# Second feed-forward of a decoder block on Trainium2: the output of hidden tiles 4 to 15 by seven block products, with three of seven low weight parts made by ScalarE and adding transfers

## The chip, the cores and the metric

One core of a Trainium2 chip runs the whole kernel. Its engines work from queues of their own and wait for each other through semaphores: TensorE (PE: matmuls out of SBUF into PSUM; PEld: its weight loads), VectorE (DVE), ScalarE (ACT), GpSimd (POOL) and SyncE (SP, which issues nearly all transfers). The metric is the device time of one execution in microseconds (us). The kernel before was timed three times: 1016.45, 1017.04 and 1017.88 us.

## The reference, cut

```python
def swiglu(u, w_in, w_out):
    a, b = jnp.split(u @ w_in, 2, axis=-1)
    return (jax.nn.silu(a) * b) @ w_out

    ...
        u = modulate(rmsnorm(h, g_norm_ffn1[l]), sh1, sc1)
        h = h + 0.5 * gt1 * swiglu(u, w_ffn1_in[l], w_ffn1_out[l])
        u = modulate(rmsnorm(h, g_norm_mix[l]), sh2, sc2)
        h = h + gt2 * token_mixing(u, cos, sin, w_in[l], w_pool[l], pool_scale[l],
                                   w_pool_branch[l], w_attn_branch[l], w_out[l])
        u = modulate(rmsnorm(h, g_norm_ffn2[l]), sh3, sc3)
        h = h + 0.5 * gt3 * swiglu(u, w_ffn2_in[l], w_ffn2_out[l])
    return rmsnorm(h, g_final)
```

There are 512 tokens of width 1024, and the hidden width of each feed-forward is 2816, all in float32. The change is in the second feed-forward alone, in the product with `w_out`, and in how the weights of its block products are split.

## The kernel before

**Layout.** Everything is held transposed: features on the 128 partitions, the 512 tokens along the row. The residual stream is eight tiles `H` of 128 x 512, the hidden layer 22 tiles.

**Three matmuls for one.** TensorE multiplies in a format with fewer bits than float32 (fp32r), so that each operand is split into a high and a low part and a product is made of three matmuls: high by high, high by low and low by high (`mm3`). For a chunk of weights ScalarE copies the raw chunk into the ring `whi` (the rounding copy is the high part), and VectorE subtracts that from the raw chunk into the ring `wlo`. A chunk has 1024 columns, 512 KB; a ring holds seven of them. The method `split` does this for the chunks in the order of `plan`, and `look(4)` ahead of each product makes sure that the chunk of four products later is in the queues. So ScalarE's and VectorE's queues hold, between the work on one product and that on the next, the split of a chunk that is needed four products later. Raw chunks come by SyncE into five buffers (`raw` and the two upper quarters of `X`).

**Input products.** From hidden tile 4 on, `duo` makes two hidden tiles at a time by Winograd's form of Strassen's scheme: seven block products (`product`, 24 matmuls of 256 columns each) in place of eight. Blocks are the two halves of the 1024 input features, the two halves (a and b of the gated unit) of the output, and the two halves of the tokens. Of the seven weight chunks three are raw ones (the first, fourth and sixth) and four are differences which VectorE makes ahead of them (`make`). A duo uses three PSUM banks A, B, C: after product 0 ScalarE copies A to C, after product 1 it copies B out (`p5`), after products 2 and 4 it copies A out (`u2`, `u3`) while A goes on being added to by products 2, 4 and 6, and after products 3 and 6 it applies silu. The hidden pair h is multiplied together in `mult`, and its high and low parts are made by `high` (ScalarE) and `low` (VectorE), which are put off by one or two products: `later(n, f)` keeps f until `step` has been called n times, and `step` comes once after each product, **ahead of** that product's own copies.

**Output products.** The hidden tiles are used up in five parts, (0, 4), (4, 8), (8, 12), (12, 16) and (16, 22) (`PARTS`). For a part other than the last, `ffn` runs eight output tiles: for each of them 4 x 3 matmuls of 512 columns, then one VectorE instruction that multiplies the bank by the gate and adds it to `H`. Four chunks of 1024 columns serve a part. The order is: part 0; pairs 4, 6 and 8, part (4, 8); pairs 10 and 12, part (8, 12); pairs 14 and 16, part (12, 16); pairs 18 and 20, the last part. So one pair of a part's successor always lies between a part's own hidden tiles and its output; it is called the third pair below.

The order of the instructions is that of the program: no scheduler moves them.

Of the kernel before, what the change touches and what calls it, by code (L numbers as in the profile page):

```python
# [14 lines left out]
P = 128  # L15
# [39 lines left out]

def lay_ffn(w_in, w_out, first, plain):

    ins, outs = [], []  # L60
    if first:
        cols = np.concatenate([c for j in range(first) for c in _tiles(j * P, DFF + j * P)])
        for k in range(KT):
            ins.append(w_in[k * P:(k + 1) * P][:, cols])
    for j in range(first, plain):
        for c in _tiles(j * P, DFF + j * P):
            ins.append(_fmajor(w_in, c))
    for j in range(plain, FT, 2):
        for i, c in ((0, 0), (0, DFF), (1, DFF), (1, 0)):
            rows = w_in[i * D // 2:(i + 1) * D // 2]  # L70
            ins.append(np.concatenate([_fmajor(rows, x) for x in _tiles(c + j * P, c + j * P + P)], axis=1))
    for k0, k1 in PARTS:
        for m in range(KT):
            outs.append(_fmajor(w_out[k0 * P:k1 * P], np.arange(m * P, (m + 1) * P)))
    n = KT * (len(PARTS) - 1)
    return ins, [np.concatenate(outs[i:i + 2], axis=1) for i in range(0, n, 2)] + outs[n:]

# [59 lines left out]
class Kernel:  # L137
# [6 lines left out]
    def plan(self):  # L144
# [11 lines left out]
        self.loads, self.order, self.last = [], [], {}  # L156
        self.shifted = set()

# [6 lines left out]

        def blocks(recs):
            n = len(self.loads)
            self.shifted.update(range(len(self.order), len(self.order) + 7))
            self.loads.extend(recs)
# [13 lines left out]
        def ffn(n, ins, outs, first):  # L183
# [4 lines left out]
            for part, (k0, k1) in enumerate(PARTS):  # L188
                while j < pairs_before(n, part):
# [5 lines left out]
                    else:  # L195
                        blocks(ins[at:at + 4])
                        j, at = j + 2, at + 4
                plain(outs[part * KT // 2:(part + 1) * KT // 2] if part + 1 < len(PARTS) else outs[-KT:])

# [71 lines left out]
    def split_hi(self):  # L271
# [21 lines left out]
        for y, x in parts:  # L293
            self.nc.scalar.activation(self.hi[:, y], r[:, x], AF.Copy)  # L294
        if i + 1 < len(self.order) and self.order[i + 1][3] and self.order[i + 1][1] < self.fetched:
            self.make(i + 1)
# [344 lines left out]
    def ffn_post(self, j, s, pb):  # L641
        nc = self.nc
        h = self.fw.tile([P, T], F32, name=("hf", "u3")[j % 2])
        nc.vector.tensor_tensor(h, s, pb, op=OP.mult)
# [4 lines left out]
    def ffn_silu(self, j, pa):  # L649
        s = self.fw.tile([P, T], F32, name=("sl", "u2")[j % 2])  # L650
        self.nc.scalar.activation(s, pa, AF.Silu)
        return s
# [70 lines left out]
    def duo(self, j, first, last):  # L723
# [12 lines left out]
        s = self.fw.tile([P, 2 * T], F32, name="sl")  # L736
        c = self.fw.tile([P, 2 * T], F32, name="hf")
        u2, u3, p5 = (self.fw.tile([P, T], F32, name=x) for x in ("u2", "u3", "p5"))
        q = lambda x: x.rearrange("p (j h t) -> p j h t", j=2, h=2)
        r = lambda x: x.rearrange("p (j t) -> p j t", j=2)  # L740
        silu = lambda h, bank: nc.scalar.activation(q(s)[:, :, h, :], r(bank), AF.Silu)

# [3 lines left out]
        def high():  # L746
            copy(self.HHall[:, j % NH * T:(j % NH + 2) * T], c)

        def low():
            x = slice(j % NH * T, (j % NH + 2) * T)  # L750
            v.tensor_tensor(self.HLall[:, x], c, self.HHall[:, x], op=OP.subtract)


        for i, (bank, u, start) in enumerate(((A, blk(lo4, T1), True), (B, S[0], True), (A, S[1], False),
                                              (C, blk(hi4, T1), False), (A, S[2], False), (B, S[3], False),
                                              (A, blk(hi4, T2), False))):
            if i == 6:
                v.tensor_tensor(q(c)[:, :, 1, :], r(u3), r(p5), op=OP.add)
            self.look(4)
# [7 lines left out]
            elif i == 1:  # L767
                copy(p5, B)
            elif i == 2:
                copy(u2, A)  # L770
            elif i == 3:
                silu(0, C)
            elif i == 4:
                copy(u3, A)
            elif i == 6:
                silu(1, A)
                v.tensor_tensor(q(c)[:, :, 0, :], r(B), r(u2), op=OP.add)
        if last:
# [3 lines left out]
        else:  # L782
            self.later(1, mult)
            self.later(2, high)
            self.later(2, low)

    def ffn2(self):
        self.put, self.now = [], 0
        bk = [self.nb() for _ in range(4)]
        self.head(2, bk, AF.Silu)  # L790
        self.todo, last = self.u_steps(2)
        do = lambda n: [self.todo.pop(0)() for _ in range(n)]
# [32 lines left out]
    def ffn(self, n, j, last=None):  # L825
# [10 lines left out]
        for part, (k0, k1) in enumerate(PARTS):  # L836
            tail = part + 1 == len(PARTS)
            while j < pairs_before(n, part):
                if j < PLAIN[n]:
                    self.ffn_pair(j, beside)  # L840
                    j += 1
                else:
                    self.duo(j, last, tail and j + 2 == FT)
                    last = None
# [3 lines left out]
            nk = k1 - k0  # L848
            hk = [(self.HH[k % NH], self.HL[k % NH]) for k in range(k0, k1)]
            if not tail:  # L850
                for m in range(0, KT, 2):
# [493 lines left out]
    def build(self):  # L1345
# [39 lines left out]
        with self.open_ffn():  # L1385
            self.ada_pool = ExitStack()
            self.adaw = self.ada_pool.enter_context(tc.tile_pool(name="f1a", bufs=4))
            self.put, self.now = [], 0
            self.startup()
# [134 lines left out]
def lay_inputs(x, c, positions, w_ada, b_ada, g_norm_ffn1, w_ffn1_in, w_ffn1_out, g_norm_mix, w_in, w_pool,  # L1524
# [3 lines left out]
    col = lambda v: A(v).reshape(-1, P).T  # L1528
    f1i, f1o = lay_ffn(A(w_ffn1_in)[0], A(w_ffn1_out)[0], FIRST, PLAIN[0])
    f2i, f2o = lay_ffn(A(w_ffn2_in)[0], A(w_ffn2_out)[0], 0, PLAIN[2])  # L1530
    wp = np.zeros((P, 2 * P), np.float32)
# [32 lines left out]
```

## Time and profile before

| | |
|---|---|
| timed runs | 1016.45, 1017.04, 1017.88 us |
| profiled execution, span from the first to the last instruction | 1018.4 us |
| second feed-forward, first block product to the last part | 734.94 to 973.61 us |
| output of a part (4 to 7, 8 to 11, 12 to 15) | 21.8 us each |
| two pairs between two outputs | 38.5 us |
| loads of a 512 KB chunk of the second feed-forward, issue to landing | 3.5 to 3.7 us |
| GpSimd busy in the second feed-forward up to its last part | 0.0 us |

The page of the profile gives of the profiled execution its span and no other time. In its rows a group of instructions has the line of the program, the engine, the operation, what it writes and reads, the count, the busy time, the mean duration of one in ns, and behind the bar the engine's idle time just ahead of them with what ended it. In a list of waits stand who waited for whom, the total, the count and the longest. In a timeline stand the start, the duration, the instruction, and in brackets the idle time before it. In a view by stretches of time each engine has its busy time and, in brackets, its instructions; then come TensorE's granted clock (1.00 is full speed), the busy share of the transfer engines and GB/s.

### The profile page before, as it was taken

The numbers are of one execution on the slowest core, as the hardware profiler recorded it, in microseconds if no ns is written. First come the engines' busy times: TensorE is split into PE (matmuls) and PEld (weight loads), VectorE is DVE, ScalarE is ACT, GpSimd is POOL, SyncE is SP. The second block draws the span as 40 slices with busy tenths as digits, with TensorE's granted clock in tenths as the row PEclk, the third lists the DMA queues.
The fourth block names the chain that finished last, engine by engine and source line by source line (L and its number), as shares of the span: only waits on it lengthen the run. The fifth ranks groups of instructions, "written<-read, shape, count | busy, mean of one in ns | idle before, by whom it ended". The sixth has DMA issues, their size and how long they took to land.

```text
span 1018.4 us, 15580 instructions
## 1 busy us (share of the span) xinstructions
PE 1007.5 (99%) x6364; PEld 913.3 (90%) x6364; DVE 756.1 (74%) x1112; ACT 437.2 (43%) x668; POOL 26.2 (3%) x30
## 2 busy tenths in 40 slices
PE   8999999999999999999999999999999999999997
PEld 7888898989999999889988888998899899998997
DVE  6979879889786776879447776577787776676764
ACT  5453352625444552233414323364366254352553
POOL 0000000000000000007100000000000000000001
PEclk9999999999999999999999999999999999999998
DMA  8856465455533413122154773312243234241312
GB/s 314 287 196 246 136 211 176 175 168 174 168 111 112 147 46 104 52 83 83 32 198 167 248 271 121 117 53 78 88 168 123 80 105 145 84 144 44 111 34 83
DMA packets 43114, 139.61 MB, mean 137 GB/s; under 512 B 4897, under 2 KB 8225, under 8 KB 43042
## 3 DMA queue, kind: packets, MB, share of 16 engines
q1 hardware_dynamic: 42354, 137.95, 40.8%
q8 instruction: 50, 0.82, 0.3%
q10 hardware_dynamic: 688, 0.66, 0.2%
q14 instruction: 22, 0.18, 0.1%
HBM read 135.82 MB, written 2.77 MB: 136 GB/s over the span
## 4 chain that ended last, share of the span: by engine, by line
PE 94%; DVE 4%; ACT 0%; issue 0%; DMA 0%; DVEq 0%; ACTq 0%
PE bank L337 17%; PE bank L338 17%; PE bank L339 17%; PE bank L719 10%; PE bank L721 10%; PE bank L720 10%; PE bank L1494 1%; PE bank L1496 1%; PE bank L1498 1%; PE bank L1090 1%; PE bank L1269 1%; PE bank L1423 1%; PE bank L1270 1%; PE bank L1271 1%; PE bank L1038 1%; DVE wlo L306 1%
## 5 line engine op out<-in xcount | busy, mean ns | idle before, releaser
L306 DVE TENSOR_TENSOR wlo<-raw,whi 128x1024 fp32r<-128x1024 f32 (+6 forms) x173 | 177.4, 1037 | 67.6 <-ACT whi L294 67.1
L294 ACT ACTIVATE whi<-raw 128x1024 fp32r<-128x1024 f32 (+6 forms) x173 | 152.3, 899 | 40.6 <-DVE raw L240 39.0
L337 PE MATMUL bank<-UH,whi 128*128 128x512 f32 (+1 forms) x432 | 158.3, 366 | 0.0
L338 PE MATMUL bank<-UL,whi 128*128 128x512 f32 (+1 forms) x432 | 154.2, 357 | 0.1
L339 PE MATMUL bank<-UH,wlo 128*128 128x512 f32 (+1 forms) x432 | 154.1, 357 | 0.0
L337 PE MATMUL bank<-HI,whi 128*128 128x512 f32 (+1 forms) x406 | 146.6, 361 | 0.0
L338 PE MATMUL bank<-HK,whi 128*128 128x512 f32 (+1 forms) x406 | 146.3, 360 | 0.0
L339 PE MATMUL bank<-HI,wlo 128*128 128x512 f32 (+1 forms) x406 | 146.2, 360 | 0.0
L721 PE MATMUL bank<-UH,wlo 128*128 128x256 f32 x512 | 141.6, 277 | 0.0
L719 PE MATMUL bank<-UH,whi 128*128 128x256 f32 x512 | 141.6, 277 | 0.0
L720 PE MATMUL bank<-UL,whi 128*128 128x256 f32 x512 | 141.6, 277 | 0.0
L306 DVE TENSOR_TENSOR wlo<-X,whi 128x1024 fp32r<-128x1024 f32 (+4 forms) x96 | 105.3, 1103 | 39.0 <-ACT whi L294 38.7
L719 PE MATMUL bank<-SH,whi 128*128 128x256 f32 x384 | 107.1, 279 | 0.1
L720 PE MATMUL bank<-SL,whi 128*128 128x256 f32 x384 | 107.0, 279 | 0.0
L721 PE MATMUL bank<-SH,wlo 128*128 128x256 f32 x384 | 106.9, 278 | 0.0
L294 ACT ACTIVATE whi<-X 128x1024 fp32r<-128x1024 f32 (+4 forms) x96 | 89.9, 958 | 32.1 <-DVE X L240 28.9
L720 PEld LDWEIGHTS bank<-UL,whi 128*128 128x128 f32 x512 | 96.3, 188 | 0.3
L719 PEld LDWEIGHTS bank<-UH,whi 128*128 128x128 f32 x512 | 96.1, 188 | 0.3
L721 PEld LDWEIGHTS bank<-UH,wlo 128*128 128x128 f32 x512 | 96.1, 188 | 0.0
L339 PEld LDWEIGHTS bank<-UH,wlo 128*128 128x128 f32 x432 | 81.3, 188 | 12.1
L338 PEld LDWEIGHTS bank<-UL,whi 128*128 128x128 f32 x432 | 81.2, 188 | 11.7 <-issue 0.5
L337 PEld LDWEIGHTS bank<-UH,whi 128*128 128x128 f32 x432 | 81.2, 188 | 11.3 <-issue 0.5
(225 smaller groups left out, 1746.4 us busy)
## 6 DMA issues: line engine op xcount, KB each, us to landing
ada<-wada SPq DMA_DIRECT2D x47, 512.0 KB, 5.0
raw<-wmix SPq DMA_DIRECT2D x44, 512.0 KB, 3.6
raw<-wf1i SPq DMA_DIRECT2D x34, 512.0 KB, 4.3
raw<-wf2i SPq DMA_DIRECT2D x30, 512.0 KB, 3.5
X<-wf2i SPq DMA_DIRECT2D x14, 512.0 KB, 3.6
cs<-wada SPq DMA_DIRECT2D x12, 512.0 KB, 3.5
AR<-wada SPq DMA_DIRECT2D x12, 512.0 KB, 4.0
raw<-wf2o SPq DMA_DIRECT2D x12, 512.0 KB, 3.6
```

Source lines behind the costliest of these rows:

```text
L294: self.nc.scalar.activation(self.hi[:, y], r[:, x], AF.Copy)
L306: self.nc.vector.tensor_tensor(self.lo[:, y], r[:, x], self.hi[:, y], op=OP.subtract)
L337: M(ps, hi, uh, start=start, stop=False)
L338: M(ps, hi, ul, start=False, stop=False)
L339: M(ps, lo, uh, start=False, stop=stop)
L719: M(o, hi, uh, start=start and p == 0 and k == 0, stop=False, skip_group_check=True)
L720: M(o, hi, ul, start=False, stop=False, skip_group_check=True)
L721: M(o, lo, uh, start=False, stop=k == 3, skip_group_check=True)
L1038: M(S[:, o + i * P:o + i * P + P], qz[:, (2 * i + h) * P:(2 * i + h + 1) * P], k[:, toks], start=True, stop=True)
L1090: M(o, pt[:, blk * P:blk * P + P], v, start=i == 0, stop=i == len(srcs) - 1)
L1269: M(b, self.UH[k][:, c::4], hi, start=k == 0, stop=False)
L1270: M(b, self.UH[k][:, c::4], lo, start=False, stop=False)
```

## The change

**Outputs.** The three parts (4, 8), (8, 12) and (12, 16) of the second feed-forward are made by `out_quad`: seven block products of 24 matmuls of 256 columns. Blocks are hidden tiles k0, k0+1 and k0+2, k0+3, the token halves, and output tiles 0 to 3 and 4 to 7. The four raw chunks of a part are laid out as blocks, and the seven weight chunks are made from them as in a duo. Each product fills two banks instead of one, so that ScalarE's copies come in twos.

**Sums of h.** The block products need four sums of the blocks of h. `h_sums` makes them in the third pair: at products 1 to 4 of that duo VectorE adds and ScalarE takes the high part, and VectorE takes the low part one product later. For that, h is kept in float32 in three buffers of two tiles (`kept`: `cond`, `cs` and `AR`, which hold nothing else by then). In the first duo of each part high and low parts are made of one token half alone.

**Low parts.** In every block of the second feed-forward, nine duos and three outputs, the first, fourth and sixth weight chunk (the raw ones) get their low part in another way: ScalarE writes the negative of the raw chunk's high part into `wlo`, and a transfer issued by GpSimd reads the raw chunk from memory once more and adds it there. VectorE's subtraction is gone for these; 36 chunks, in 48 transfers, since a chunk that crosses the end of the ring is cut in two.

```diff
+        if i in self.outer:
+            name, off, w = self.loads[self.outer[i]]
+            src = self.a[name][off:off + P * w].rearrange("(p n) -> p n", p=P)
+            for y, x in parts:
+                self.nc.scalar.activation(self.lo[:, y], r[:, x], AF.Copy, scale=-1.0)
+            for y, x in parts:
+                self.nc.gpsimd.dma_start(self.lo[:, y], src[:, x], accum_op=OP.add)
+            parts = []
...
+        ts = slice(0, 1 if self.kept and j % 4 == 0 and j < PARTS[-1][0] else 2)
...
+        for n, what in enumerate(((lambda: add(h22, h21, h22, OP.add), lambda: high(0, h22)),
+                                  (lambda: add(h21, h11, h21, OP.subtract), lambda: high(2, h21), lambda: low(0, h22)),
+                                  (lambda: add(h11, h22, h11, OP.subtract), lambda: high(1, h11), lambda: low(2, h21)),
+                                  (lambda: add(h12, h12, h11, OP.subtract), lambda: high(3, h12), lambda: low(1, h11)),
+                                  (lambda: low(3, h12),))):
+            for f in what:
+                self.later(2 + n, f)
...
+        def product(banks, u, start):
+            w = self.take()
+            for m in range(4):
+                o = banks[m // 2][:, m % 2 * HT:m % 2 * HT + HT]
+                for k in range(2):
+                    (hi, lo), (uh, ul) = w[2 * m + k], u[k]
+                    M(o, hi, uh, start=start and m % 2 == 0 and k == 0, stop=False, skip_group_check=True)
+                    M(o, hi, ul, start=False, stop=False, skip_group_check=True)
+                    M(o, lo, uh, start=False, stop=k == 1, skip_group_check=True)
...
+        for i, (bank, u, start) in enumerate(((A, blk(k0, T1), True), (B, G[0], True), (A, G[1], False),
+                                              (C, blk(k0 + 2, T1), False), (A, G[2], False), (B, blk(k0, T2), False),
+                                              (A, blk(k0 + 2, T2), False))):
...
                 else:
+                    if self.kept and not tail and j == k1:
+                        self.h_sums(k0)
                     self.duo(j, last, tail and j + 2 == FT)
...
+            if not tail and part and n:
+                self.out_quad(k0, gate)
+                continue
```

**The order in the first third pair** (tiles 8 and 9, ahead of the output of tiles 4 to 7). ScalarE before, from the copy of product 0 to the copy of product 4; `bank`, `p` and `u` are the duo's copies, `sl` its silu, `whi` the high part of a weight chunk, `HI` that of h:

```order
L726 ACTIVATE bank_97<-bank_101 128x512
L294 ACTIVATE whi<-X 128x1024
L726 ACTIVATE HI<-hf 128x1024
L726 ACTIVATE p_6564<-bank_102 128x512
L294 ACTIVATE whi<-X 128x1024
L726 ACTIVATE u_6562<-bank_101 128x512
L294 ACTIVATE whi<-raw_68 128x896
L294 ACTIVATE whi<-raw_68 128x128
L741 ACTIVATE sl<-bank_97 128x2x256
L294 ACTIVATE whi<-raw_66 128x1024
L726 ACTIVATE u_6563<-bank_101 128x512
```

The high part of h (`HI`) stands ahead of the copy `p` of product 1, and otherwise one chunk's high part stands between a product's copy and the next. ScalarE in the change, from the copy of product 0 to that of product 2; `wlo` is the negative, `ut` the high part of a sum of h:

```order
L745 ACTIVATE bank_97<-bank_101 128x512
L305 ACTIVATE whi<-X 128x1024
L310 ACTIVATE wlo<-X 128x1024
L745 ACTIVATE HI<-cond 128x1024
L830 ACTIVATE ut<-cond 128x512
L745 ACTIVATE p_6570<-bank_102 128x512
L305 ACTIVATE whi<-X 128x1024
L830 ACTIVATE ut<-AR 128x512
L745 ACTIVATE u_6571<-bank_101 128x2x256
```

A negative and the high part of a sum now stand ahead of the copy of product 1, and the high part of a further sum ahead of the copy of product 2. ScalarE goes on, to the copy of product 4:

```order
L305 ACTIVATE whi<-raw_68 128x896
L305 ACTIVATE whi<-raw_68 128x128
L310 ACTIVATE wlo<-raw_68 128x896
L310 ACTIVATE wlo<-raw_68 128x128
L830 ACTIVATE ut<-AR 128x512
L768 ACTIVATE sl<-bank_97 128x2x256
L305 ACTIVATE whi<-X 128x1024
L830 ACTIVATE HI<-cond 128x2x256
L745 ACTIVATE u_6571<-bank_101 128x2x256
```

One negative in two pieces and the high parts of two sums were added ahead of the copy of product 4. VectorE in the change in the same stretch; line 779 is the low part of h, line 325 that of a weight chunk, line 827 a sum of h, line 833 the low part of a sum, and line 251 a difference of weights:

```order
L779 TENSOR_TENSOR HK<-cond,HI 128x1024
L827 TENSOR_TENSOR cond<-AR,cond 128x2x256
L325 TENSOR_TENSOR wlo<-X,whi 128x1024
L827 TENSOR_TENSOR AR<-AR 128x2x256
L833 TENSOR_TENSOR G_5879<-cond,ut 128x512
L251 TENSOR_TENSOR X<-raw_66,raw_68 128x1024
L827 TENSOR_TENSOR AR<-cond,AR 128x2x256
L833 TENSOR_TENSOR G_5883<-AR,ut 128x512
L251 TENSOR_TENSOR X<-raw_67,X 128x1024
L325 TENSOR_TENSOR wlo<-X,whi 128x1024
L827 TENSOR_TENSOR cond<-cond,AR 128x2x256
L833 TENSOR_TENSOR G_5881<-AR,ut 128x512
```

Each sum but the first of these stands behind a weight chunk's low part or a difference of weights, in the order in which `look` and `step` put them into the queue.

More of the change, by code (lines that the diff above doesn't have):

```diff
@@ L53, in _tiles, with lay_ffn @@
     return [np.arange(s, s + P) for s in starts]
-def lay_ffn(w_in, w_out, first, plain):
+def lay_ffn(w_in, w_out, first, plain, blocks):
     ins, outs = [], []
@@ L195, in ffn @@
                     else:
-                        blocks(ins[at:at + 4])
+                        blocks(ins[at:at + 4], n == 2)
                         j, at = j + 2, at + 4
-                plain(outs[part * KT // 2:(part + 1) * KT // 2] if part + 1 < len(PARTS) else outs[-KT:])
+                put = blocks if n and 0 < part < len(PARTS) - 1 else plain
+                put(outs[part * KT // 2:(part + 1) * KT // 2] if part + 1 < len(PARTS) else outs[-KT:],
+                    **({"outer": True} if put is blocks else {}))
         ffn(0, f1i, f1o, FIRST)
@@ L773, in duo @@
             elif i == 4:
-                copy(u3, A)
+                copy(u3, r(A))
             elif i == 6:
                 silu(1, A)
-                v.tensor_tensor(q(c)[:, :, 0, :], r(B), r(u2), op=OP.add)
+                v.tensor_tensor(q(c)[:, :, 0, :], r(B), u2, op=OP.add)
         if last:
```

106 lines of the change are left out of this document (90 added, 16 removed).

## The prediction

> **What bounds the kernel now.** I read the busy shares first, then the chain of waits, then the second feed-forward by stretches of time.
>
> ```profile
> span 1018.4 us, 15580 instructions
> PE 1007.5 (99%) x6364; PEld 913.3 (90%) x6364; DVE 756.1 (74%) x1112; ACT 437.2 (43%) x668; POOL 26.2 (3%) x30
> ...
> PE 94%; DVE 4%; ACT 0%; issue 0%; DMA 0%; DVEq 0%; ACTq 0%
> ...
> core 0: us, PE busy (x) PEld busy (x) DVE busy (x) ACT busy (x) POOL busy (x), PEclk, DMA share, GB/s
> ...
> 792.67:814.45 21.78, 21.78 (x98) 18.03 (x97) 15.19 (x17) 6.72 (x8) 0.00 (x0) 1.00 0.19 58
> 814.45:852.98 38.53, 38.53 (x337) 38.52 (x336) 28.07 (x29) 20.04 (x27) 0.00 (x0) 1.00 0.41 135
> 852.98:874.77 21.79, 21.79 (x99) 18.03 (x97) 15.19 (x16) 6.63 (x7) 0.00 (x0) 1.00 0.18 53
> ```
>
> The last three rows are the output of tiles 4 to 7, two pairs of input tiles (14 block products), and the output of tiles 8 to 11. TensorE is busy for the whole of each at full granted clock, and 94% of the chain is matmuls: every matmul slot saved is time saved, and every wait of TensorE is time lost. Output: 96 matmuls of 512 columns, 21.78/96 = 0.227 us a slot. Block products: 336 of 256 columns, 38.53/336 = 0.1147 us, so 24 of them, one product, take 2.75 us. VectorE is busy for 28.07 of 38.53 us and ScalarE for 20.04. The waits of 735 to 974 us say what those two wait for:
>
> ```profile
> DVE wlo L306 <- ACT whi L294: 42.2, 38, 1.8
> ACT sl L741 <- PE bank L721: 37.3, 18, 3.3
> ACT bank L726 <- PE bank L721: 26.7, 9, 5.2
> ACT u L726 <- PE bank L721: 20.1, 18, 1.3
> ```
>
> TensorE stands in none of that list's rows as the one waiting: ScalarE follows TensorE, VectorE follows ScalarE, and only the work ahead (four products) keeps that circle from closing on TensorE.
>
> **The change part by part.** *Matmuls.* Each of three outputs loses 96 slots of 512 columns and gains 7 x 24 = 168 of 256: 21.78 - 168 x 0.1147 = 21.78 - 19.27 = 2.5 us saved, 7.5 us for three. Weight loads keep up: 336 beside 336 matmuls above.
>
> *Engine time.* The rows of 735 to 974 us by shape, and one from the whole span:
>
> ```profile
> L306 DVE TENSOR_TENSOR wlo<-raw,whi 128x1024 fp32r<-128x1024 f32 x22 | 26.9, 1223 | 12.8 <-ACT whi L294 12.8
> L294 ACT ACTIVATE whi<-raw 128x1024 fp32r<-128x1024 f32 x21 | 22.0, 1053 | 15.4 <-DVE raw L240 15.4
> L863 DVE SCALAR_TENSOR_TENSOR H<-bank,mod,H 128x512 f32<-128x512 f32 x25 | 18.5, 749 | 20.0 <-PE bank L339 20.0
> L240 DVE TENSOR_TENSOR X<-raw,X 128x1024 f32<-128x1024 f32 x13 | 15.8, 1219 | 0.0
> L726 ACT ACTIVATE u<-bank 128x512 f32<-128x512 f32 x18 | 10.8, 599 | 20.1 <-PE bank L721 20.1
> L751 DVE TENSOR_TENSOR HK<-hf,HI 128x1024 fp32r<-128x1024 f32 x8 | 9.7, 1219 | 0.0
> L726 ACT ACTIVATE HI<-hf 128x1024 fp32r<-128x1024 f32 x8 | 8.4, 1052 | 14.7 <-DVE hf L744 14.7
> L758 DVE TENSOR_TENSOR hf<-u,p 128x512 f32<-128x512 f32 x9 | 6.2, 686 | 0.0
> L294 ACT ACTIVATE whi<-raw 128x896 fp32r<-128x896 f32 x6 | 5.7, 943 | 0.0
> L294 ACT ACTIVATE whi<-raw 128x128 fp32r<-128x128 f32 x6 | 1.8, 298 | 0.0
> ...
> L489 DVE SCALAR_TENSOR_TENSOR H<-bank,mod,H 128x256 f32<-128x256 f32 x24 | 11.6, 482 | 9.2 <-PE bank L339 9.0
> ```
>
> One output with its two pairs, 60.3 us before. VectorE loses three lows in each pair's seven chunks (6 x 1.22 = 7.3), eight updates of H (6.0) and half of one low of h (0.5). It gains four weight differences (4.9), four sums of h with four lows and four adds of product parts (12 x 0.69 = 8.2), eight updates of 256 columns (3.9) and four of 512 (3.0); four weight lows stay. Net 20.0 - 13.8 = +6.2 on 43.3 busy: 49 of 57.8 us. ScalarE gains nine negatives (9.5), three more high parts (3.2), four highs of h and eight copies (12 x 0.6 = 7.2), less half of one high (0.5): 26.7 + 19.4 = 46. Both still fit under TensorE's 57.8, so by totals this is free (were VectorE the bound, its 6.2 would be the price of an output, 18.6 in all). The three buffers for h and the new order of banks add no instruction. The order of the queues decides.
>
> *The wait that is new.* In the third pair the sums of h run one step a product. In each step VectorE adds and ScalarE takes the high part, queued **ahead of** ScalarE's copy of the product just done; the add is queued behind a weight low, which waits for the weight's high on ScalarE, which is behind the previous copy. That is a closed loop. Its hand-overs, here from the pair starting at 814.45, and a pair of highs back to back:
>
> ```profile
> 817.48 0.58 ACT L726 ACTIVATE bank<-bank 128x512 f32<-128x512 f32 x1 [5.20 <-PE bank L721]
> 817.98 1.05 ACT L294 ACTIVATE whi<-raw 128x1024 fp32r<-128x1024 f32 x1
> 820.36 0.60 ACT L726 ACTIVATE p<-bank 128x512 f32<-128x512 f32 x1 [1.33 <-PE bank L721]
> ...
> 768.72 2.00 ACT L294 ACTIVATE whi<-X 128x1024 fp32r<-128x1024 f32 x2
> ...
> 815.32 1.22 DVE L306 TENSOR_TENSOR wlo<-raw,whi 128x1024 fp32r<-128x1024 f32 x1
> 816.45 1.22 DVE L240 TENSOR_TENSOR X<-raw,X 128x1024 f32<-128x1024 f32 x1
> 819.06 1.23 DVE L306 TENSOR_TENSOR wlo<-raw,whi 128x1024 fp32r<-128x1024 f32 x1 [1.39 <-ACT whi L294]
> ```
>
> Product 0 ends at 814.45 + 2.75 = 817.20, and its copy starts 0.28 later. On ScalarE the next instruction starts 0.50 after a copy and 0.95 after a high; on VectorE 1.13 after a low; a hand-over takes 0.03 (819.03 to 819.06). Times from the end of product 0, along the order rows of the change: copy 0.28, weight high 0.78, negative 1.73, high of h 2.68 (ends 3.73), its low 3.76, first sum 4.89 (ends 5.58), its high 5.61, copy of product 1 6.11, weight high 6.61 (ends 7.66), low 7.69, second sum 8.82 (ends 9.51), its high 9.54, copy of product 2 10.04 (ends 10.64). Product 4 adds onto the bank which that copy reads, so it starts at 10.67 instead of 3 x 2.75 = 8.25: **2.4 us**. On: two highs (896 and 128 columns) 10.54 and 11.38, two negatives 11.58 and 12.42, high 12.62, silu 13.12, weight high 13.62 (ends 14.67), low 14.70, last sum 15.83 (ends 16.52), high 16.55, copy of product 4 17.05 (ends 17.65). Product 6 needs that bank and was due at 10.67 + 5.50 = 16.17: **1.5 us**. So 3.9 us an output, 11.7 for three. Its bounds: with 0.1 less on each of eight hand-overs and starts, 3.1 (9.3 in all); with 0.1 more, 4.7 (14.1). The other pairs and the output block lack the sums, so their copies follow their products.
>
> *The adding transfers*, 36 chunks: in none of the rows of before. GpSimd issues each after the negative; behind a waiting one stand only further ones, and the matmuls of that chunk's low part wait for it. Bounds come from loads and from GpSimd's own work:
>
> ```profile
> raw<-wf2i SPq DMA_DIRECT2D x30, 512.0 KB, 3.5
> ...
> L1150 POOL TENSOR_TENSOR rt<-rt 128x527 f32<-128x527 f32 (+4 forms) x6 | 8.4, 1396 | 3.2 <-DVE wlo L306 2.2 <-ACT rt L1144 0.6
> ```
>
> Below, 3.5 us as a load. Above, two loads in turn (the destination is read as well) and 1.4 us to issue: 8.4. Cover: a chunk is taken up when the copy of a product is done and used four products later, so 11.0 + 0.23 (two matmuls) - 0.4 - 0.5 - 0.95 - 1.05 = 8.3 us. I take 6, midway, which is hidden. [...] DMA share: 1.57 MB more in 19.3 us is 81 GB/s, counted twice 163, on 135 GB/s at 0.41: about 0.9 at worst. Loads of raw weights keep their number; their buffers come free earlier. The middle chunk of a block's three is taken up a product earlier, since product 5 leaves no copy on ScalarE. So each microsecond beyond 8.3 holds TensorE at up to two chunks of each of 12 blocks, 24 us; half of that if each delay gives the next chunk air.
>
> Sum: -7.5 + 11.7 = **+4.2**, and 0.8 for loads that share the queue's engines (0 to 3). The profiled span, 1018.4, is 1.4 above the median 1017.0, in which the difference is taken: 1022.
>
> **The rivals.** *A, the loop does not stop TensorE* (faster): then 1017.0 - 7.5 = 1009.5, or 1013 with 1.2 us a part. For it: VectorE and ScalarE have 20% free. Against it: a step of the loop (copy to copy, 6.11 to 10.04) is 3.9 us long against 2.75 of a product. Chance 0.12. *B, transfers late* (slower still): it decides from 8.3 us on; at 9 us, 0.7 x 12 = 8 to 0.7 x 24 = 17 on top of the loop: 1030 to 1039. For it: the share of 0.9. Against it: 6 is well short of 8.3. Chance 0.27. *C, waits and savings cancel* (the lower bound, 9.3 - 7.5, and no dearer loads): 1018.8, chance 0.09. *D, the chunks wait but not for transfers: raw loads come late to the differences*: as B in size, 0.02.
>
> **How the numbers follow.** Forecast 0.50 (1019.5 to 1026). Slower by over 0.2% (2 us, about what this measurement can tell): 0.50 + 0.27 + 0.02 = 0.79; within 0.2%: 0.09; faster: 0.12. Range 1016 to 1036: it leaves out A and the upper third of B.
>
> **What would show it.** Per output, 168 matmuls of 256 columns in 19.3 us. In each third pair, two waits of TensorE on ScalarE's copy of the products' bank, 2.4 and 1.5 us, at products 4 and 6, three times; none in the other pairs. No wait of TensorE on the adding transfers, landing about 6 us after issue. It is wrong if TensorE has no such wait (A) or if the low parts of chunks 1, 4 and 6 of a block hold it (B).

## The result, and the profile after

| | before | after |
|---|---|---|
| median of timed runs, us | 1017.38 (1016.45 to 1017.88, 4 runs) | 1035.11 (1033.96 to 1035.45, 4 runs) |
| ratio to before, 95% interval | | 1.0165 (1.015 to 1.0181) |
| span of the profiled execution, us | 1018.4 | 1033.3 |
| first block product of the second feed-forward to its last part, us | 238.67 | 256.54 |

The change makes the kernel slower by 17.7 us. The stretch in which it lies is longer by 17.9 us, so that all of it is there. The spans differ by 14.9 only, because the work ahead of that stretch, which is the same in both, ended 3.15 us earlier in the second profile. Of the fourteen profiles of this case, five have TensorE at full clock from 19 to 20 us on and start the stretch at 734.5 to 735.2 us; the other nine first have full clock at 10 to 12 us and start it at 730.9 to 732.8. The timed runs of the kernel before lie apart in the same way, at 1016.2 to 1017.9 and at 1019.6 to 1020.0 us, so that the median of a few runs can be off by some 3 us. Below, medians stand for the kernel and stretches for the parts.

The head of the page after, with the shares of the chain that ended last:

```profile
span 1033.3 us, 16222 instructions
PE 1006.7 (97%) x6580; PEld 921.4 (89%) x6580; DVE 760.9 (74%) x1134; ACT 497.6 (48%) x762; POOL 68.5 (7%) x78
...
PE 78%; issue 9%; DMA 6%; DVE 4%; POOL 1%; ACT 1%; POOLq 0%; DVEq 0%; ACTq 0%
```

Matmuls fell from 94% of that chain to 78%. In their place stand transfers (6%) and "issue", time in which the engine waited for nothing that the profile shows. TensorE is busy for as long as before and the span is longer: it now stands still. The list of its waits, 700 to 1000 us, which had no row before:

```profile
PE bank L738 <- ACT u L745: 6.9, 3, 2.3
PE bank L740 <- DMA wlo<-wf2i: 4.7, 4, 2.7
PE bank L866 <- DMA wlo<-wf2o: 3.5, 3, 1.9
```

The first row is the forecast wait on ScalarE's copy, three times. The other two are the adding transfers, 8.2 us in seven waits, of which the forecast had none. By stretches of time (three pairs, then output and two pairs in turn):

```profile
core 0: us, PE busy (x) PEld busy (x) DVE busy (x) ACT busy (x) POOL busy (x), PEclk, DMA share, GB/s
731.79:799.50 67.71, 62.36 (x505) 61.77 (x504) 41.13 (x42) 42.50 (x59) 9.65 (x11) 0.95 0.71 171
799.50:820.96 21.46, 19.51 (x170) 19.32 (x169) 17.16 (x21) 15.03 (x22) 4.38 (x5) 1.00 0.85 188
820.96:864.47 43.51, 40.73 (x339) 40.33 (x337) 31.04 (x37) 28.92 (x40) 6.15 (x7) 0.96 0.70 162
864.47:884.89 20.42, 19.51 (x171) 19.32 (x170) 17.07 (x21) 15.03 (x22) 4.39 (x5) 1.00 0.85 190
884.89:929.30 44.41, 40.92 (x338) 40.49 (x337) 31.24 (x37) 28.93 (x40) 6.17 (x7) 0.96 0.69 163
929.30:949.84 20.54, 19.86 (x170) 19.66 (x169) 17.37 (x21) 15.55 (x22) 4.38 (x5) 1.00 0.83 187
949.84:988.33 38.49, 38.49 (x338) 38.49 (x337) 26.51 (x31) 24.02 (x33) 4.37 (x5) 1.00 0.72 174
```

The three outputs save 0.3, 1.4 and 1.2 us against 21.8 before, instead of 2.5 each. Two pairs with a third pair among them take 43.51 and 44.41 us in place of 38.53. The last two pairs, which have neither sums of h nor a late transfer, take 38.49 as before. The column before the DMA share shows something else: a granted clock of 0.95 and 0.96, which the kernel before has nowhere in this stretch. Three stretches of 3.41 us in the view by windows, TensorE alone, show what it is:

```profile
786.99:790.40 3.41, 1.12 (x9) 1.00 0.63 125
790.40:793.81 3.41, 3.41 (x19) 0.50 0.39 54
793.81:797.22 3.41, 3.41 (x31) 1.00 0.98 201
```

In the first of them TensorE waits for 2.29 us; the next passes at half clock, with 19 matmuls in it or across its ends in place of 31, which loses some 1.7 us (half of 3.41); then full clock is back. The records have four such windows, at 749.4, 790.4, 855.3 and 920.1 us, each behind a wait of 2.3 to 2.7 us.

### The profile page after: what moved, and what is told of

It reads as the page before. It is cut to its first block, busy times and chain, and to the rows that moved or that the text cites. A ratio compares the mean times of both kernels' runs of the same rounds, so it can differ in the third digit from the quotient of the medians.

```text
span 1033.3 us, 16222 instructions
## 1 busy us (share of the span) xinstructions
PE 1006.7 (97%) x6580; PEld 921.4 (89%) x6580; DVE 760.9 (74%) x1134; ACT 497.6 (48%) x762; POOL 68.5 (7%) x78
## 4 chain that ended last, share of the span: by engine, by line
PE 78%; issue 9%; DMA 6%; DVE 4%; POOL 1%; ACT 1%; POOLq 0%; DVEq 0%; ACTq 0%
PE bank L356 15%; PE bank L357 15%; PE bank L358 15%; PE bank L740 7%; PE bank L738 7%; PE bank L739 7%; DMA wlo<-wf2i 4%; DMA wlo<-wf2o 3%; PE bank L1615 1%; PE bank L1619 1%; PE bank L1617 1%; PE bank L1211 1%; POOL wlo L312 1%; PE bank L1390 1%; PE bank L1391 1%
## 5 line engine op out<-in xcount | busy, mean ns | idle before, releaser
L325 DVE TENSOR_TENSOR wlo<-raw,whi 128x1024 fp32r<-128x1024 f32 (+6 forms) x144 | 148.9, 1044 | 60.2 <-ACT whi L305 59.9
L325 DVE TENSOR_TENSOR wlo<-X,whi 128x1024 fp32r<-128x1024 f32 (+2 forms) x87 | 100.1, 1152 | 64.2 <-ACT whi L305 63.9
L738 PE MATMUL bank<-SH,whi 128*128 128x256 f32 x384 | 109.7, 286 | 6.9 <-ACT u L745 6.9
L305 ACT ACTIVATE whi<-X 128x1024 fp32r<-128x1024 f32 (+4 forms) x104 | 99.5, 975 | 26.6 <-DVE X L251 25.2
L356 PE MATMUL bank<-HI,whi 128*128 128x512 f32 (+1 forms) x310 | 109.2, 352 | 0.0
L739 PE MATMUL bank<-SL,whi 128*128 128x256 f32 x384 | 109.2, 284 | 0.0
L740 PE MATMUL bank<-SH,wlo 128*128 128x256 f32 x384 | 109.2, 284 | 0.0
L357 PE MATMUL bank<-HK,whi 128*128 128x512 f32 (+1 forms) x310 | 108.9, 351 | 0.0
L358 PE MATMUL bank<-HI,wlo 128*128 128x512 f32 (+1 forms) x310 | 108.9, 351 | 0.0
L357 PEld LDWEIGHTS bank<-UL,whi 128*128 128x128 f32 x432 | 81.2, 188 | 11.7 <-issue 0.5
```

Of the source, the lines that this page charges most:

```text
L325: self.nc.vector.tensor_tensor(self.lo[:, y], r[:, x], self.hi[:, y], op=OP.subtract)
L356: M(ps, hi, uh, start=start, stop=False)
L357: M(ps, hi, ul, start=False, stop=False)
L358: M(ps, lo, uh, start=False, stop=stop)
L738: M(o, hi, uh, start=start and p == 0 and k == 0, stop=False, skip_group_check=True)
L739: M(o, hi, ul, start=False, stop=False, skip_group_check=True)
```

## The experiments

Where a kernel was timed, the kernel before was timed beside it on the same chip (1017.15 to 1017.27 us in the three sets). The stretch, first block product of the second feed-forward to its last part, is that of the one execution that was profiled.

| | median, us | ratio to before, 95% interval | stretch in the profile, us |
|---|---|---|---|
| before (first set) | 1017.20 | | 238.67 |
| the change | 1035.11 | 1.0165 (1.015 to 1.0181) | 256.54 |
| copies ahead of the sums | 1034.19 | 1.0152 (1.0125 to 1.0179) | 256.74 |
| no adding transfers | 1026.18 | 1.0083 (1.0051 to 1.0115) | 244.93 |
| transfers alone | 1023.87 | 1.0057 (1.004 to 1.0075) | 243.96 |
| waits of rising length in the kernel before | 1034.19 (one run) | | 256.58 |
| plain transfers | 1021.59 | 1.0036 (1.002 to 1.0053) | 244.50 |
| wait filled with matmuls | 1036.16 | 1.0174 (1.0147 to 1.0202) | 254.99 |
| copies ahead, no transfers | 1018.13 | 1.001 (0.9995 to 1.0024) | 239.65 |
| sums spread, two transfers a block | 1013.08 | 0.9949 (0.993 to 0.9968) | 232.90 |
| the change with two transfers a block | 1023.70 | 1.0053 (1.0036 to 1.007) | 242.42 |
| sums spread, three transfers | 1026.95 | 1.0089 (1.0064 to 1.0114) | 243.72 |
| sums spread, three transfers, five ahead | 1012.70 | 0.9952 (0.9933 to 0.9971) | 234.86 |
| sums spread, no transfers | 1011.89 | 0.9944 (0.9926 to 0.9962) | 233.39 |

**Copies ahead of the sums.** In the third pairs `step` comes after the product's own copies.

```diff
             self.product(bank, u, start)
-            self.step()
+            if not self.late:
+                self.step()
...
                 v.tensor_tensor(q(c)[:, :, 0, :], r(B), u2, op=OP.add)
+            if self.late:
+                self.step()
```

> In the third pairs alone, ScalarE's copies of a product go into the queue ahead of the sums of h and not behind them. Queue theory (the copies of the products wait behind the high part of a sum, which waits for VectorE): the three waits of TensorE on that copy, 2.3 us each, go, and with them the three stretches of half clock behind them, 2 us each, so about 13 us less than the change, 1022 us; if the transfers, which those waits had covered, now come late in the outputs, some 4 us of it are given back: 1018 to 1026 us. Rival (VectorE and ScalarE are full in the third pair, whatever the order): TensorE waits about as long at another product, and the time stays within 3 us of the change's 1035 us.

1034.19 us, no gain, which is in the rival's range, though VectorE and ScalarE aren't the reason. TensorE's waits, 700 to 1000 us:

```profile
PE bank L869 <- DMA wlo<-wf2o: 8.1, 6, 2.4
PE bank L740 <- DMA wlo<-wf2i: 5.2, 5, 2.5
PE bank L738 <- ACT u L745: 2.6, 5, 0.8
```

The order of ScalarE's queue does make the wait on its copy (6.9 to 2.6 us). But TensorE, which comes earlier now, waits for the transfers instead (8.2 to 13.3 us). One loss hid behind the other, so that curing this one alone shows nothing.

**No adding transfers.** All low parts go back to VectorE; the outputs by block products stay.

```diff
-            if outer:
-                self.outer.update({len(self.order): n, len(self.order) + 3: n + 3, len(self.order) + 5: n + 2})
```

> All low parts by VectorE's subtraction again; the outputs stay seven block products. Theory (the waits on the adding transfers, 8.3 us in the trace, and one stretch of half clock, 2 us, come from the transfers alone): 1035 - 10 = about 1025 us, with the three waits of about 2.3 us on ScalarE's copies still there and the half clock behind each. Rival (without the transfers VectorE is the bound, its 3.7 us a block come back): VectorE over 95% busy between 735 and 990 us, TensorE waits for low parts of weights, 1035 us or more.

1026.18 us, as expected. All three outputs took 19.03 to 19.05 us. The one row of TensorE's waits, and the two pairs ahead of the second and the third output:

```profile
PE bank L736 <- ACT u L743: 9.9, 6, 2.2
```

```profile
816.26:859.63 43.37, 40.57 (x338) 40.18 (x337) 38.95 (x46) 23.42 (x32) 0.00 (x0) 0.96 0.29 98
878.67:922.02 43.35, 38.97 (x338) 38.57 (x337) 38.94 (x46) 23.41 (x32) 0.00 (x0) 1.00 0.30 98
```

The first of these has a window at half clock and a second wait, at product 6, of 0.56 us; the second has full clock and a second wait of 2.15. They last equally long: half clock gives ScalarE the time for which TensorE would have waited two products later. In the loop of the third pair half clock therefore cost next to nothing by itself.

**Transfers alone.** The kernel before, its outputs with plain products, and adding transfers for three chunks of each of the second feed-forward's nine blocks of input products.

```diff
+        if i in self.outer:
+            name, off, w = self.loads[self.outer[i]]
+            src = self.a[name][off:off + P * w].rearrange("(p n) -> p n", p=P)
+            for y, x in parts:
+                self.nc.scalar.activation(self.lo[:, y], r[:, x], AF.Copy, scale=-1.0)
+            for y, x in parts:
+                self.nc.gpsimd.dma_start(self.lo[:, y], src[:, x], accum_op=OP.add)
+            parts = []
...
-                        blocks(ins[at:at + 4])
+                        blocks(ins[at:at + 4], n == 2)
```

> The kernel before with the adding transfers in the nine input pairs alone; outputs by plain products of 512 columns, no sums of h. Theory (a transfer takes about 8 us from its issue, against a cover of 7.6 to 8.5): waits on transfers in some pairs, 3 to 6 us in all with at most one stretch of half clock, 1020 to 1024 us. Rival (the transfers are late only because the outputs' copies and sums delay the negatives): no wait on a transfer, 1017 us as before, landing unchanged at about 7 us or shorter.

1023.87 us, as expected. TensorE waits for transfers although nothing else was changed:

```profile
PE bank L731 <- DMA wlo<-wf2i: 3.5, 3, 2.6
```

So the transfers are late by themselves. (The stretch is 5.3 us longer, and the three waits are 3.5 of it; most of the rest isn't assigned.) Its longest wait, 2.58 us, brought no half clock; it fell on two windows of 3.41 us, 1.39 us on one and 1.19 on the other.

**Waits of rising length.** The kernel before, with spare copies on ScalarE ahead of its copy of product 2 in six pairs, more from pair to pair.

```diff
             elif i == 2:
+                for w in self.stall.get(j, ()):
+                    copy(self.cond[:, :w], A[:, :w])
                 copy(u2, A)
...
+        self.stall = {6: [T] * 4 + [256], 8: [T] * 5 + [P], 10: [T] * 6, 12: [T] * 6 + [P],
+                      14: [T] * 6 + [384], 16: [T] * 7 + [384]}
```

> The kernel before with spare copies by ScalarE ahead of its copy of product 2 in six pairs, so that TensorE waits once in each, about 1.0, 1.6, 1.9, 2.2, 2.5 and 3.1 us. Nothing else is changed; the output stays right. Clock theory (a wait of TensorE above about 2 us is followed by 3.4 us at half clock): the waits of 1.0, 1.6 and 1.9 leave the granted clock at 1.00, the other three are each followed by one stretch at 0.5 and cost some 2 us beyond themselves: 12.3 + 6 + 1 = about 19 us more than before. Rival (half clock comes from something else in the change, such as two banks at a time or the transfers' traffic): the clock stays at 1.00 all through and the time rises by the waits alone, about 13 us.

One run, 1034.19 us, 17.0 over the kernel before beside it. The waits were 0.77, 1.35, 1.61, 1.98, 2.13 and 2.82 us:

```profile
PE bank L719 <- ACT u L726: 10.7, 6, 2.8
```

Half clock followed on the last three and not on the first three, always for one stretch of 3.41 us. The wait of 1.98 us, with the stretch behind it:

```profile
846.23:849.65 3.42, 1.44 (x13) 1.00 0.00 0
849.65:853.06 3.41, 3.41 (x18) 0.50 0.41 112
```

Between the three stretches the clock was full for 40.96 and 20.48 us, 12 and 6 times 3.413. Here no second wait stood behind, and the half clock comes on top of the waits: 10.7 + 3 x 1.7 = 15.8 of the 17.

**Plain transfers.** GpSimd's 36 chunks without adding.

```diff
-                self.nc.gpsimd.dma_start(self.lo[:, y], src[:, x], accum_op=OP.add)
+                self.nc.gpsimd.dma_start(self.lo[:, y], src[:, x])
```

> The changed kernel with GpSimd's 36 chunks transferred without adding: the same issues, bytes and places, but the raw weights overwrite the negatives, so the low parts of those chunks are wrong. Theory (the adding makes a transfer land 7.1 to 7.7 us after its issue, at the edge of the 8.3 us that cover it): landing falls to 3.5 to 5 us, the 8.2 us of TensorE's waits on transfers go, and with them their one stretch at half clock (2 us) and some restarts (about 1 us); the 6.9 us of waits on ScalarE stay: 1023 to 1026. Rival (issuing from GpSimd or the busy queues make it 7 us, adding or not): landing stays near 7 us, the waits stay, 1033 to 1036.

1021.59 us, below the expected 1023 to 1026. TensorE's waits, and the least, median and greatest time to landing of GpSimd's transfers from 725 to 985 us, first of the change and then of this kernel:

```profile
PE bank L738 <- ACT u L745: 10.9, 6, 2.3
PE bank L740 <- DMA wlo<-wf2i: 0.4, 1, 0.4
```

```profile
DMA to landing us min/median/max: 5.0/7.3/10.1
```

```profile
DMA to landing us min/median/max: 3.6/4.7/7.8
```

Here adding cost 2.6 us in the median (7.3 against 4.7), with the same issues and places. Without it the transfers' waits are gone but for 0.4 us, no window between 17 and 1016 us is at half clock, and now the second wait is there, 1.33 us at product 6 behind 2.30 at product 4. This kernel has all the rest of the change, and its time is that of the forecast's sum (1022.0).

**The wait filled with matmuls.** In each third pair 20 matmuls that nobody reads, behind product 3.

```diff
             self.product(bank, u, start)
+            if i == 3 and self.warm:
+                for _ in range(20):
+                    nc.tensor.matmul(self.B[7][:, :HT], self.UH[0][:, :P], self.UH[1][:, T1], start=True, stop=True)
             self.step()
```

> The changed kernel with 20 more matmuls of 256 columns into a bank that nobody reads, behind product 3 of each third pair: 20 x 0.1147 = 2.3 us of TensorE work in the place of its wait of 2.3 us. Theory (a window of the clock with about 1.8 us of idle TensorE is followed by one at half clock, about 2 us dearer): the three half-clock stretches behind those waits, at 790, 855 and 920 us, go (-6 us), and since they gave ScalarE time, the forecast's second wait, up to 1.5 us at product 6, comes in their place (up to +4.5): 1029 to 1034. Rival (the half clock has another cause): it stays in those places, no second wait, 1034 to 1037.

1036.16 us, in the rival's range; its runs lie far apart (1032.18 to 1040.25). Its trace shows what the theory said, though, in TensorE's waits and in the clock:

```profile
PE bank L869 <- DMA wlo<-wf2o: 4.8, 3, 2.1
PE bank L740 <- DMA wlo<-wf2i: 4.3, 5, 2.5
PE bank L738 <- ACT u L745: 3.8, 3, 1.3
```

```profile
core 0: 1035.1 us, clock 0.998
```

No window between 20 and 1030 us is at half clock, and the second wait, 1.32, 1.32 and 1.12 us at product 6, has taken its place; the stretch is 255.0 us long against 256.5. So the half clock behind those three waits went when 20 matmuls took the place of the idle time, and being rid of it bought 1.5 us in the stretch of one profile and nothing that the times show.

**Copies ahead, no transfers.** The first two experiments together.

> Both experiments together: ScalarE's copies of the products ahead of the sums in the third pairs, and all low parts by VectorE. Theory (two separate losses, the loop in the third pair and the late transfers): outputs at 19.04 us save 8.2 us of 1017.2, waits on ScalarE fall from 9.9 us to the 2.6 that were left with copies first, no half clock: 1010 to 1014. Rival (VectorE has too little room without the transfers, 6 us more an output, so the low parts of weights or of h come late instead): VectorE's waits move to TensorE, 1018 to 1026.

1018.13 us, in the rival's range, though not by its mechanism. The row of TensorE's waits:

```profile
PE bank L736 <- ACT u L743: 5.5, 7, 1.3
```

The wait at product 6 of the third pair (1.30 us each time) stays, with 0.32 to 0.39 at product 4; the seventh wait, 0.56 us, is in the first pair behind the last output. With the copies first the sums still come one a product, each two hand-overs between VectorE and ScalarE long; whoever goes first, a wait stays (2.2 us at the longest with the sums first, 1.3 here), so that the loop is still longer than a product. The theory had missed that: the order of copy and sum was half of the wait (9.9 to 5.5 us), the density of the sums the other half (5.5 us to none on ScalarE in the last experiment below).

**Sums spread, two transfers a block.** Copies first in third pairs and outputs, the sums of h at steps 3, 4, 6, 8 and 10, and no adding transfer for the chunk of product 5.

```diff
-                self.outer.update({len(self.order): n, len(self.order) + 3: n + 3, len(self.order) + 5: n + 2})
+                self.outer.update({len(self.order): n, len(self.order) + 3: n + 3})
...
-                self.later(2 + n, f)
+                self.later((3, 4, 6, 8, 10)[n], f)
```

> A version meant to beat both: copies of the products ahead of the steps in the third pairs and in the outputs, the sums of h at every second product (steps 3, 4, 6, 8, 10 instead of 2 to 6), and adding transfers for two of a block's chunks instead of three, not for the middle one, which is taken up a product earlier. Theory (order and number of transfers are the cause, not the block products themselves): waits on ScalarE under 1 us each, waits on transfers under 3 us in all, no half clock: 1010 to 1015, faster than before. Rival (two transfers a block still land after their cover, and each wait of some 2 us brings half clock): 1018 to 1026.

The chunk that was left out is the sixth of a block (product 5, counted from 0); "taken up a product earlier", here and in the next expectation, is true of the fourth, not of it. 1013.08 us, faster than before. TensorE's waits:

```profile
PE bank L869 <- DMA wlo<-wf2o: 0.6, 2, 0.4
PE bank L740 <- DMA wlo<-wf2i: 0.2, 1, 0.2
```

**The change with two transfers a block.** That one edit alone.

> The changed kernel with one edit: a block's middle chunk (the fourth product's successor but one, taken up a product earlier than the others) gets its low part from VectorE, so two adding transfers a block instead of three. Theory (the transfers are late because they last 7 us against a cover that is shortest for the middle chunk, and the more of them the later): waits on transfers fall from 8.2 to under 3 us, the waits on ScalarE stay at about 3.6 an output, as with plain transfers: 1019 to 1025. Rival (any adding transfer of 7 us holds TensorE): waits on transfers of 5 us or more, 1029 to 1035.

1023.70 us, as expected. TensorE's waits, and an output with the two pairs behind it:

```profile
PE bank L738 <- ACT u L745: 10.7, 6, 2.2
```

```profile
793.21:812.25 19.04, 19.04 (x171) 19.04 (x169) 17.34 (x22) 14.33 (x21) 3.51 (x4) 1.00 0.68 167
812.25:854.76 42.51, 38.96 (x338) 38.57 (x337) 33.80 (x39) 27.08 (x38) 4.39 (x5) 1.00 0.63 149
```

24 adding transfers are left and none is waited for. Leaving out 12 of 36 gives back 11.4 us in the medians and 14.1 in the stretch. The trace of the change shows why those 12: counted in matmuls, all its seven waits on transfers stand at product 5. GpSimd's issues of the fourth and of the sixth chunk of the first output, and the time to landing of each:

```profile
799.83 0.86 POOL L312 DMA_DIRECT2D wlo<-wf2o  x1 [6.24 <-PE bank L740]
805.53 0.87 POOL L312 DMA_DIRECT2D wlo<-wf2o  x1 [4.83 <-ACT wlo L310]
```

```profile
DMA to landing us min/median/max: 5.6/5.6/5.6
DMA to landing us min/median/max: 9.9/9.9/9.9
```

The second is wanted by the third matmul of product 5, which would have started at 813.33 us (the second one starts at 813.21), 7.8 after the issue; it lands at 815.44. What ran on the transfer engines during the one (800.7 to 805.4 us) and, in the second list, during the other (806.4 to 815.4), by queue with packets, MB and the share of the 16 engines' time, q0 being GpSimd's queue and q1 SyncE's loads:

```profile
q0 software_dynamic: 144, 0.52, 69.3%
q1 hardware_dynamic: 48, 0.20, 12.2%
```

```profile
q1 hardware_dynamic: 400, 1.46, 59.0%
q0 software_dynamic: 188, 0.68, 39.0%
```

The first has the engines nearly to itself. The second shares them with the loads of raw weights, which take 59% of their time, and takes 4.3 us longer. (The 0.68 MB of q0 take in part of the next chunk's transfers, issued from 810.82 us on.) Of the transfers issued in the stretch, the fourth chunks' landed in 5.0 to 5.8 us, with loads at 0 to 11% of the engines' time between issue and landing; the sixth chunks' landed in 7.8 to 10.1, with loads at 45 to 66%. The first chunks', most of them in two pieces, took 6.3 to 9.3 and were never waited for; the three longest stood behind a wait for a sixth chunk, which gave them time. Plain transfers show the same split, 3.6 to 4.2 us for the fourth and 5.8 to 7.8 for the sixth. (That the loads are the cause is read from these shares; no run moved them.)

**Sums spread, three transfers.** The version above with all 36 transfers.

> The version with the spread sums and copies first, now with all three transfers a block. Theory (two separate losses: the order cures the waits on ScalarE, the middle chunk's transfer stays late): no wait on ScalarE over 0.5 us, waits on transfers of 6 to 13 us in all with half clock behind the long ones: 1022 to 1032. Rival (the transfers were late only because the loop delayed ScalarE's negatives): waits on transfers under 3 us, 1010 to 1015.

1026.95 us, as expected. No wait on ScalarE is left, and no half clock followed, against the theory; the transfers' waits are:

```profile
PE bank L869 <- DMA wlo<-wf2o: 6.1, 6, 2.1
PE bank L740 <- DMA wlo<-wf2i: 3.7, 3, 2.6
```

The longest wait, 2.58 us, again fell on two windows, 1.38 and 1.20 us. The order of the sums does not make the transfers come in time.

**The same, five ahead.** In the second feed-forward every `look(4)` becomes `look(5)`.

```diff
-            self.look(4)
+            self.look(5 if self.kept else 4)
```

> As the run before, with weights taken up five products ahead instead of four in the second feed-forward: 2.75 us more cover, 11 us against 7.1 to 7.7 us of landing; nothing else changes. Theory (it is cover against landing): no wait on transfers but the first one near 749 us, where the second block's chunks are taken up as before: 1012 to 1020. Rival (the transfers hold one another up on their queue, or there is no room to take a chunk up earlier): waits as with four ahead, 1022 to 1032.

1012.70 us: 14.3 us less than the run before for 2.75 us more cover. In the stretch it is 8.9 us (243.72 to 234.86); 3.5 us lie ahead of the stretch, where the two kernels do the same. TensorE's only wait, and the times to landing:

```profile
PE bank L740 <- DMA wlo<-wf2i: 2.6, 1, 2.6
```

```profile
DMA to landing us min/median/max: 5.1/7.4/10.9
```

The transfers last as long as ever; it is cover against landing. The one wait left is the one expected, at product 5 of the first pair that has a late transfer (748 us).

**Sums spread, no transfers.** All low parts by VectorE.

> The version with the spread sums and copies first, without any adding transfer: all low parts by VectorE. Theory (what the transfers free on VectorE is not needed once the sums are spread: 49 + 12 x 1.22 - 4.9, some 59 us of work on an output's 57.6 us of TensorE, so it is just full): small waits on VectorE or ScalarE of 1 to 3 us an output against 2.7 saved: 1012 to 1019. Rival (VectorE is full and its lateness reaches TensorE in every pair): 1020 to 1030.

1011.89 us, just below the expected 1012. TensorE's waits, and an output with the two pairs behind it in one stretch:

```profile
PE bank L866 <- DVE G L834: 0.8, 3, 0.3
```

```profile
788.62:847.12 58.50, 58.22 (x507) 58.03 (x505) 57.60 (x69) 35.59 (x51) 0.00 (x0) 1.00 0.33 109
```

VectorE is busy for 57.60 of 58.50 us and TensorE hardly waits for it. The adding transfers free time on VectorE that the version with spread sums does not need. This, the version with five ahead and the one with two transfers cannot be told apart by their intervals; all three beat both kernels.

## Why the prediction was right in direction and short in size

**Slots saved: right.** Forecast 2.5 us an output; outputs that wait for nothing took 19.04 us, 2.74 less than 21.78, or 8.2 us for three against 7.5.

**The new loop: right.** Forecast 2.4 us at product 4 and 1.5 at product 6. Where nothing else interferes (two transfers, plain transfers) it was 2.23 to 2.30 and 1.32 us, 10.7 to 10.9 for three outputs against 11.7. In the changed kernel only the first stands in the list (2.29 or 2.30, three times), because the window at half clock behind it gives ScalarE the time for the second. Rival A, that the loop does not stop TensorE, fell; nor did a fuller engine stop TensorE: VectorE was busy for 98% (57.60 of 58.50 us) with the sums spread and no transfers.

**The adding transfers: the step that failed.** The prediction took one duration for all of them, 6 us, midway between 3.5 and 8.4, held it against a cover of 8.3, and put the term at 0. The cover was about right (7.8 us where it was measured). The duration was right for none of the chunks that matter: 5.0 to 5.8 us with the engines nearly free, 7.8 to 10.1 beside loads, so that the upper bound of 8.4 was passed too. The same part worked out a share of the transfer engines of up to 0.9, but the sum used it only for 0.8 us of dearer loads, not for the transfers themselves, whose lateness it left to rival B.

**What lateness costs.** It is rival B's mechanism at its own place, the low parts of a block's chunks, but at one chunk of a block, not at up to two, with waits of 0.3 to 2.7 us. The measured 1035.1 lies in B's 1030 to 1039, partly by luck: B has waits alone on top of the loop, 8 to 17 us, and the waits were 8.2. With the late chunk out, the stretch is 242.4 us, 3.75 over before, where the forecast's sum has 4.2. With it, 256.5: 14.1 more. Of that 8.2 us are the waits; four windows at half clock are 6.8, less the 3.8 of second waits on ScalarE that they hide (10.7 less 6.9); four more stops of TensorE, at some 0.27 each beyond the wait shown, are 1.1 (from start to start 2.56 us pass at a wait of 2.29, and 0.22 at the next matmul, where 0.11 is usual). These make 12.3; the other 1.8 us are not assigned.

**The clock: missing.** No term of the sum and no rival had it, since before shows no wait in this stretch that could have shown it.

**VectorE: right.** The 49 us foreseen (17.16 and 31.04 measured, for the first output and the two pairs behind it) left room under TensorE's 57.8, enough even for all the low parts.

## What to carry to other kernels

A transfer that must land before a deadline is best priced chunk by chunk, with what else is on the transfer engines at that moment: here the same 512 KB took 5.0 us with loads at 0% of the engines' time and 10.1 us with loads at some 65% in one kernel, and only the slowest of each block set the time. Where a change adds two possible losses, cure them together before judging either: putting the copies first gave 0.9 us with the adding transfers in place and 8.1 without them (1026.18 to 1018.13; by stretches, a loss of 0.2 and a gain of 5.3). And work that goes through two engines in turns wants to be spread until a round trip fits between two turns: at one sum a product, 2.75 us apart, the forecast's round trip of 3.9 us did not fit, and at one every second product no wait on ScalarE was left. Taking load off VectorE did not help here: the waits on ScalarE were 9.9 us without adding transfers and 10.7 with two a block.

## What the runs showed of the hardware that was not expected

**The clock's windows.** In the trace of the change the granted clock falls to half at 749.44, 790.40, 855.25 and 920.10 us, for 3.413 us each time. The times at full clock ahead of the four falls, 737.28, 37.55, 61.44 and 61.44 us, are 216, 11, 18 and 18 times that; in the kernel before, the one time at full clock, 993.28 us, is 291 times that. Windows are here such lengths of 3.413 us, counted from where the clock becomes full. Between 700 and 1000 us of these traces, a window in which TensorE idled for 1.98 us (waits of rising length) or more was followed by one at half clock in all twelve cases; at 1.84 it was once (copies ahead of the sums), at 1.93 once not (plain transfers); at 1.79 (no adding transfers) and below never. What decides between 1.79 and 1.98 us is not shown. Waits of the same length had two prices: 2.58 us lay in two windows in the transfers alone (1.39 and 1.19 us) and with the sums spread and three transfers (1.38 and 1.20), and no half clock followed; with five ahead 2.58 us lay in one, and the next passed at half clock.

**Small adding transfers.** A piece of 64 KB took about as long as one of 512 KB: 7.3 us against 7.1 in the medians of the changed kernel. It is issued right behind one of 448 KB, and no run had it by itself, so what it costs alone stays open.
